# A decoder layer on one core: the queue that issues the transfers of the stored operands

## The chip, the cores and the metric

The kernel runs on one core of one Trainium2 chip. The metric is the device time of one execution in microseconds (us). The core has TensorE (PE in the profile; its weight loads are PEld), VectorE (DVE), ScalarE (ACT) and GpSimd (POOL). SyncE (SP) computes nothing here and issues most transfers. SP and GpSimd each issue transfers in the order of their own queue. An instruction at the head of a queue that waits for a semaphore holds up all that stand behind it.

## The reference

One layer of a hybrid decoder in float32, on x of 1024 tokens by 1024 features, with a memory of 256 tokens:

```
h = LN1(alpha*x + 0.5 * (silu(x@wg1) * (x@wu1)) @ wd1)      # FFN 1, inner width 2816
h = LN2(alpha*h + [HGRN2(h) ; spatial_gate(h)] @ w_out)      # token mixers
h = LN3(alpha*h + attention(h, LN(mem)) @ xa_w_o)            # 4 heads, 256 memory tokens
out = LN4(alpha*h + 0.5 * (silu(h@wg2) * (h@wu2)) @ wd2)     # FFN 2, the same form
```

## The kernel before

Every matmul operand is split into a rounded high part (ACT, L114) and a low remainder (DVE, L115), and each product is three matmuls: high by high, low by high and high by low (`mm3`, L137 to L139). Each FFN runs through its 22 column blocks of 128 in pairs. For a pair it loads four 512 KB weight tiles, two of the gate (`wg_f_r`) and two of the up projection (`wu_f_r`), and forms sums of them on DVE (L498 to L501), because each projection is done with seven block products in place of eight (`strassen`). A pair is thus 14 products of 12 matmuls of 128x128 by 128x512. The results leave PSUM through ACT (L528, L531, L533) and DVE, and SP stores combinations of them in DRAM (`lops`, L626 to L629). The next pair's weights are loaded and split while this pair is multiplied. A raw weight tile has 3 buffers (tag `raw`), a high part 6 (tag `whi`) and a low part 5.

Beside the pairs of FFN 1 runs a flow of its own, `later` (L926), which makes ready what later stages read: 14 tiles for the output projection of attention (`sq_xa`, called items 0 to 13 here) and 4 tiles of FFN 2's weights (`f_ops`). The flow is `prepare` (L281). For each item it does this, and then rests for 16 us of the program's own reckoning, in which a product counts as 2.6 us:

- the raw tile is in a buffer of which there is one (`load`, L283, tag `pre`, tiles `pr_xa` and `pr_f`);
- ACT writes its high part `ph_xa` (L293) and the negative of that, `pn_xa` (L294), both into buffers of the tag `whi`, the pool from which the weights of the pairs take theirs;
- both are stored to DRAM (L296), and the next item's raw tile is loaded (L286);
- an adding transfer adds the raw operand in DRAM onto the stored negative, which leaves the low part (L301);
- for items 0 to 7, a step of the sums of blocks follows (`square_operands`, L261): an even item copies one 512x512 block to a sum in DRAM, and the next odd item adds another block to it, each in two halves (L269). The sums 7, 6, 4 and 5 are made in this order; sum 6 begins as a copy of sum 7, and sum 4 as a copy of sum 6. Later items load these sums as raw tiles.

`pinned` keeps instructions of one engine in the program's order. The rest is placed by a scheduler, which sets the order of every queue when the kernel is built. All transfers of `prepare` but the loads of the four FFN 2 tiles stand on GpSimd's queue. There are 16 `nc.gpsimd.dma_start` halves at L269, 14 loads at L286, 36 stores at L296 and 30 adding transfers at L301, each of 512 KB or of a part of that. The weight loads, and all else, stand on SP's queue.

Of the kernel before, what the change touches and what calls it, by code (L numbers as in the profile page):

```python
# [8 lines left out]
F32 = mybir.dt.float32  # L9
# [25 lines left out]
def hybrid_layer_kernel(ctx: ExitStack, tc: tile.TileContext, a, out):  # L35
    nc = tc.nc
# [10 lines left out]
    def gt(name, shape=(P, 1024), dtype=F32):  # L47
        return gpool.tile(list(shape), dtype, tag="g", name=name)
# [209 lines left out]
    pinned = tc.keep_in_program_order  # L258
    probe = {}

    def square_operands(w, ops, name):  # L261

        wb = w.rearrange("(kb k) (db d) -> kb db k d", kb=2, db=2)
        sums, steps = {}, []
        halves = [slice(i * 2 * P, (i + 1) * 2 * P) for i in range(2)]

        def step(dst, src, **op):
            for rows in halves:
                pinned(nc.gpsimd.dma_start(dst[rows], src[rows], **op))  # L269

        for p, b in ((1, (0, 0)), (2, (1, 0)), (3, (1, 1))):
            sums[p] = wb[b[0], b[1]]
        for p, first, b in ((7, 3, (0, 1)), (6, 7, (0, 0)), (4, 6, (1, 0)), (5, 1, (0, 1))):
            sums[p] = dram.tile([HALF, HALF], F32, name=f"sum_{name}{p}")
            steps.append(partial(step, sums[p], sums[first]))
            steps.append(partial(step, sums[p], wb[b[0], b[1]], accum_op=ALU.add))
        todo = [(sums[p][2 * n * P:2 * (n + 1) * P].rearrange("(i p) d -> p i d", p=P), ops[p - 1, n],
                 f"{name}_{p}{n}") for p in (1, 2, 3, 7, 6, 4, 5) for n in range(2)]
        return todo, steps

    def prepare(todo, steps):  # L281

        def load(k):  # L283
            src, _, name = todo[k]
            raw = wpool.tile(list(src.shape), F32, tag="pre", bufs=1, name=f"pr_{name}")
            pinned((nc.gpsimd if src.shape[1] == 2 else nc.sync).dma_start(raw, src))  # L286
            return raw

        raw = load(0)
        yield 16  # L290
        for k, (src, dst, name) in enumerate(todo):
            hi, neg = (wpool.tile(list(src.shape), F32R, tag="whi", bufs=6, name=f"p{i}_{name}") for i in "hn")
            pinned(nc.scalar.activation(hi, raw, AF.Copy))  # L293
            pinned(nc.scalar.activation(neg, hi.bitcast(F32), AF.Copy, scale=-1.0))  # L294
            for d, t in zip(dst, (hi, neg)):
                pinned(nc.gpsimd.dma_start(d, t.bitcast(F32)))  # L296
            if k + 1 < len(todo):
                raw = load(k + 1)
            for i in range(0, src.shape[1], 2):
                part = slice(i, i + 2)  # L300
                pinned(nc.gpsimd.dma_start(dst[1][:, part], src[:, part], accum_op=ALU.add))  # L301
            if steps:
                steps.pop(0)()
            yield 16

    def fetch_parts(src, name):
        hi = wpool.tile(list(src[0].shape), F32R, tag="whi", bufs=6, name=f"{name}_h")
# [323 lines left out]
    def down(wd, res_src, gb, bb, dst, make_xT, name):  # L631
# [73 lines left out]
        def pair(ps, when):  # L705

            bank = {p: [(ps_tr if j and t > 1 else ps_mm)(f"dp_{name}_{p}_{t}") for t in range(4)]
                    for j, p in enumerate(ps)}
            for k, _ in steps(ps):
                ahead(3)  # L710
                rh, rl, lh, ll = ready.pop((ps, k))
                for j, p in enumerate(ps):
                    l = SLOT[p] - min(SLOT[q] for q in ps)
                    for t in range(4):
                        ts = slice(t * P, (t + 1) * P)
                        mm3(bank[p][t], lh[:, l, ts], ll[:, l, ts], rh[:, j, :], rl[:, j, :],
                            k == 0, k == nk - 1)
                tick(5.2)
                if k in when:
                    prepare(when[k])  # L720
            ahead(2)
            return [bank[p] for p in ps]
# [203 lines left out]
    def later():  # L926
        yield 40

        pinned(nc.gpsimd.tensor_scalar(sm("begun", [P, 1]), probe["b"], 1.0, None, op0=ALU.mult))
        todo, steps = [], []  # L930
        for n, w in (("xa", a["xa_w_o"][0]),):
            t, s = square_operands(w, sq_ops[n], n)
            todo += t
            steps += s
        todo += [(wcol(w, f), f2_ops[i, f], f"f2{i}{f}") for f in range(2)
                 for i, w in enumerate((a["ffn2_w_gate"][0], a["ffn2_w_up"][0]))]
        yield from prepare(todo, steps)
# [451 lines left out]
    for j in range(2):  # L1389
        for i, (hi, lo) in enumerate(((kTh[j].rearrange("p c m -> p (c m)"),  # L1390
                                       kTl[j].rearrange("p c m -> p (c m)")), (vmh[j], vml[j]))):
            t = gt(f"kv{i}{j}")
# [72 lines left out]
```

## Time and profile before

| | |
|---|---|
| Time, median of 3 runs | 2069.17 us (2065.11 to 2072.62) |
| The profiled execution's own time | 2069.69 us |
| Its span, first to last instruction | 2068.0 us |
| PE busy | 2017.1 us (98%) |
| DVE, ACT and POOL busy | 1488.4, 916.2 and 176.8 us |
| Mean granted TensorE clock | 0.989 |
| Queue of SP (q1) | 315.75 MB |
| Queue of GpSimd (q0) | 44.05 MB |

In a row of the timeline stand the start, the duration, the engine, the line and what is written from what. In brackets stands how long the engine sat idle before it, and which instruction's end let it go; "issue" there means that the profile shows nothing that it waited for. In the table of waits stand the total, the number of waits and the longest one. Buffer numbers are left out of the names, so that FFN 1 and FFN 2 both appear as `f`; FFN 1's pairs lie between 62 and about 520 us.

### The profile page before, as it was taken

How to read it: one execution, taken by the hardware profiler on the slowest of the kernel's cores; microseconds unless marked ns; L12 is line 12 of the kernel's file. 1: busy time of each engine (PE TensorE's matmuls, PEld its weight loads, DVE VectorE, ACT ScalarE, POOL GpSimd, SP SyncE). 2: the span in 40 equal slices, each digit the busy share in tenths (PEclk: the TensorE clock that was granted, in tenths of full speed). 3: DMA queues.
4: the chain of work that ended last, by engine and by line, in shares of the span. 5: the costliest groups of instructions: out<-in, count | busy, mean ns of one | idle time of the engine just before them, and what ended most of it. 6: DMA issues, size and time to landing. Idle time of an engine off the chain costs nothing.

```text
span 2068.0 us, 25498 instructions
## 1 busy us (share of the span) xinstructions
PE 2017.1 (98%) x9598; PEld 1686.4 (82%) x9598; DVE 1488.4 (72%) x2238; ACT 916.2 (44%) x1279; POOL 176.8 (9%) x245
## 2 busy tenths in 40 slices
PE   8999879999999999999999999999999999999998
PEld 8888658878787888888888888888888888888886
DVE  5977456748767876785797765478776776776688
ACT  6634334434343537746754434334423333344442
POOL 0011221120000220100011100001000000000021
PEclk9999989999999999999999999999999999999999
DMA  8369987855877753123225643464233332377874
GB/s 262 116 200 254 248 226 211 244 158 168 302 266 274 258 163 87 50 82 90 64 84 189 226 130 115 165 244 162 87 113 97 97 114 95 107 240 280 290 264 167
DMA packets 265371, 361.41 MB, mean 175 GB/s; under 512 B 16224, under 2 KB 160224, under 8 KB 265184
## 3 DMA queue, kind: packets, MB, share of 16 engines
q1 hardware_dynamic: 247008, 315.75, 45.7%
q0 software_dynamic: 18240, 44.05, 8.9%
q8 instruction: 75, 1.23, 0.2%
q14 instruction: 48, 0.39, 0.1%
HBM read 267.99 MB, written 109.58 MB: 183 GB/s over the span
## 4 chain that ended last, share of the span: by engine, by line
PE 68%; DVE 3%; DMA 1%; issue 1%; POOL 1%; ACT 0%; SPq 0%; POOLq 0%; DVEq 0%; ACTq 0%
PE dp_f L137 6%; PE dp_f L138 5%; PE dp_f L139 5%; PE st_gf L138 3%; PE st_uf L138 3%; PE st_uf L137 3%; PE st_gf L137 3%; PE st_gf L139 3%; PE st_uf L139 3%; PE psl L1167 2%; PE paq L137 1%; PE paq L138 1%; PE paq L139 1%; PE acc_mx L137 1%; PE acc_mx L139 1%; PE acc_mx L138 1%
## 5 line engine op out<-in xcount | busy, mean ns | idle before, releaser
L138 PE MATMUL dp_f<-wd_f_l,ah_f 128*128 128x512 f32 x552 | 214.3, 391 | 0.0
L137 PE MATMUL dp_f<-wd_f_h,ah_f 128*128 128x512 f32 x552 | 209.6, 392 | 3.9 <-ACT ah_f L114 3.9
L139 PE MATMUL dp_f<-wd_f_h,al_f 128*128 128x512 f32 x552 | 206.1, 390 | 0.6 <-DVE al_f L115 0.6
L137 PEld LDWEIGHTS dp_f<-wd_f_h,ah_f 128*128 128x128 f32 x552 | 104.2, 189 | 26.1 <-ACT ah_f L114 4.7
L139 PEld LDWEIGHTS dp_f<-wd_f_h,al_f 128*128 128x128 f32 x552 | 103.6, 188 | 22.7 <-DVE al_f L115 1.5
L138 PEld LDWEIGHTS dp_f<-wd_f_l,ah_f 128*128 128x128 f32 x552 | 104.2, 189 | 21.7
L114 ACT ACTIVATE wd_f_h<-wd_f_r 128x1024 fp32r<-128x1024 f32 x72 | 73.1, 1021 | 94.3 <-DVE wd_f_r L650 35.7
L114 ACT ACTIVATE ah_f<-ar_f 128x1024 fp32r<-128x1024 f32 x72 | 73.3, 1020 | 71.4 <-DMA ar_f<-lops 67.2
L115 DVE TENSOR_TENSOR al_f<-ar_f,ah_f 128x1024 fp32r<-128x1024 f32 x72 | 84.5, 1174 | 27.8 <-ACT ah_f L114 27.3
L115 DVE TENSOR_TENSOR wd_f_l<-wd_f_r,wd_f_h 128x1024 fp32r<-128x1024 f32 x72 | 84.2, 1174 | 10.7 <-ACT wd_f_h L114 10.7
L115 DVE TENSOR_TENSOR wu_f_l<-wu_f_r,wu_f_h 128x1024 fp32r<-128x1024 f32 x42 | 51.2, 1219 | 47.6 <-ACT wu_f_h L114 47.6
L137 PE MATMUL st_uf<-xh,wu_f_h 128*128 128x512 f32 x168 | 66.3, 394 | 14.0 <-ACT wu_f_h L114 14.0
L774 POOL TENSOR_SCALAR nm_f<-nm_f 128x1 f32<-128x1 f32 x8 | 10.6, 1330 | 780.8 <-ACT xl L773 780.8
L114 ACT ACTIVATE wu_f_h<-wu_f_r 128x1024 fp32r<-128x1024 f32 x42 | 44.1, 1051 | 49.6 <-issue 31.0
L138 PE MATMUL st_uf<-xl,wu_f_h 128*128 128x512 f32 x168 | 65.9, 392 | 0.0
L137 PE MATMUL st_gf<-xh,wg_f_h 128*128 128x512 f32 x168 | 65.4, 389 | 0.0
L138 PE MATMUL st_gf<-xl,wg_f_h 128*128 128x512 f32 x168 | 65.4, 389 | 0.0
L139 PE MATMUL st_uf<-xh,wu_f_l 128*128 128x512 f32 x168 | 64.9, 390 | 0.0
L139 PE MATMUL st_gf<-xh,wg_f_l 128*128 128x512 f32 x168 | 64.7, 389 | 0.0
L530 DVE TENSOR_TENSOR top_uf<-bot_uf,st_uf 128x512 f32<-128x512 f32 x21 | 14.4, 687 | 59.4 <-PE st_uf L139 46.7
L114 ACT ACTIVATE wg_f_h<-wg_f_r 128x1024 fp32r<-128x1024 f32 x42 | 44.2, 1052 | 21.9 <-PE st_gf L138 15.1
L115 DVE TENSOR_TENSOR wg_f_l<-wg_f_r,wg_f_h 128x1024 fp32r<-128x1024 f32 x42 | 51.2, 1220 | 3.2 <-ACT wg_f_h L114 2.9
(504 smaller groups left out, 6015.5 us busy)
## 6 DMA issues: line engine op xcount, KB each, us to landing
ar_f<-lops SPq DMA_DIRECT2D x66, 512.0 KB, 5.3
wd_f_r<-in_ffn_w_down_dram SPq DMA_DIRECT2D x56, 512.0 KB, 5.0
wg_f_r<-in_ffn_w_gate_dram SPq DMA_DIRECT2D x42, 512.0 KB, 3.8
wu_f_r<-in_ffn_w_up_dram SPq DMA_DIRECT2D x42, 512.0 KB, 3.9
wd_mx_r<-in_w_out_dram SPq DMA_DIRECT2D x24, 512.0 KB, 4.2
lops<-bot_gf SPq DMA_DIRECT2D x21, 512.0 KB, 2.8
lops<-top_uf SPq DMA_DIRECT2D x21, 512.0 KB, 4.5
lops<-bot_uf SPq DMA_DIRECT2D x21, 512.0 KB, 5.1
```

What stands on the lines that cost most here:

```text
L114: order(nc.scalar.activation(hi, src, AF.Copy))
L115: order(nc.vector.tensor_tensor(lo, src, hi.bitcast(F32), op=ALU.subtract))
L137: nc.tensor.matmul(ps, lh, rh, start=first, stop=False, skip_group_check=more)
L138: nc.tensor.matmul(ps, lh, rl, start=False, stop=False, skip_group_check=more)
L139: nc.tensor.matmul(ps, ll, rh, start=False, stop=last, skip_group_check=more)
L530: nc.vector.tensor_tensor(t0, b0, product(2), op=ALU.add)
L774: nc.gpsimd.tensor_scalar(nmean, nmean, -1.0 / D, None, op0=ALU.mult)
L1167: nc.tensor.matmul(psl[:m, (i * NC2 + c) * 64:(i * NC2 + c + 1) * 64] .rearrange("p (n b) -> p n b", b=B), e[:, :m], blk(e, B)[:, :, 1, :] ...
```

## The change

GpSimd keeps the adding transfers alone, at L269 and L301. The plain copies of the sums, all loads of raw tiles and the stores of both parts go to SP's queue. Between ACT's two conversions and the stores the flow now rests for 4, and at the end of an item for 12 instead of 16. Behind L294 the changed kernel's line numbers are one higher.

```diff
         def step(dst, src, **op):
             for rows in halves:
-                pinned(nc.gpsimd.dma_start(dst[rows], src[rows], **op))
+                pinned((nc.gpsimd if op else nc.sync).dma_start(dst[rows], src[rows], **op))
...
-            pinned((nc.gpsimd if src.shape[1] == 2 else nc.sync).dma_start(raw, src))
+            pinned(nc.sync.dma_start(raw, src))
...
             pinned(nc.scalar.activation(neg, hi.bitcast(F32), AF.Copy, scale=-1.0))
+            yield 4
             for d, t in zip(dst, (hi, neg)):
-                pinned(nc.gpsimd.dma_start(d, t.bitcast(F32)))
+                pinned(nc.sync.dma_start(d, t.bitcast(F32)))
...
             if steps:
                 steps.pop(0)()
-            yield 16
+            yield 12
```

In the built program 58 transfers move from GpSimd's queue to SP's: 36 stores, 14 loads and 8 half copies. The order of PE's instructions is the same as before; on ACT and DVE a few neighbours of FFN 1 change places.

The first place is GpSimd's queue in the items 7 to 9. `sum_xa_1188` is sum 5, and a wait for DMASW is a wait for an earlier transfer of GpSimd, one for DMAHW for one of SP, one for Activation for ACT. Before:

```order
L296 DMA sq_xa<-ph_xa_2193 128x1024 [waits DMASW3_49,Activation_49]
L296 DMA sq_xa<-pn_xa_2194 128x1024 [waits DMASW4_49,Activation_49]
L286 DMA pr_xa_2199<-sum_xa_1186 128x2x512 [waits DMASW7_49,DMASW5_49]
L301 DMA sq_xa<-sum_xa_1185 256x1x512 [waits DMASW4_49]
L269 DMA sum_xa_1188<-in_xa_w_o_dram 256x512 [waits DMASW1_49]
L269 DMA sum_xa_1188<-in_xa_w_o_dram 256x512 [waits DMASW2_49,DMASW0_49]
L296 DMA sq_xa<-ph_xa_2329 128x1024 [waits Activation_49]
L296 DMA sq_xa<-pn_xa_2330 128x1024 [waits Activation_49]
L286 DMA pr_xa_2335<-sum_xa_1186 128x2x512 [waits DMASW5_49,DMASW3_49]
```

The same queue now, at the same items:

```order
L302 DMA sq_xa<-sum_xa_1185 256x1x512 [waits DMAHW1_49,DMASW5_49]
L269 DMA sum_xa_1188<-in_xa_w_o_dram 256x512 [waits DMAHW4_49,DMASW6_49]
L269 DMA sum_xa_1188<-in_xa_w_o_dram 256x512 [waits DMAHW5_49,DMASW7_49]
L302 DMA sq_xa<-sum_xa_1186 256x1x512 [waits DMAHW7_49,DMASW0_49]
L302 DMA sq_xa<-sum_xa_1186 256x1x512 [waits DMAHW5_49,DMASW1_49]
```

The stores of items 7 and 8 and the load of item 9, the last row of the fence before, no longer stand behind the two halves that are added to sum 5. They are now on SP's queue, whose rows at item 8 are these:

```order
L123 DMA wg_f_12_1_r<-in_ffn_w_gate_dram 128x8x128 [waits DMAHW6_49,DMAHW4_49,DVE_49]
L297 DMA sq_xa<-ph_xa_2329 128x1024 [waits DMAHW5_49,Activation_49]
L630 DMA lops<-top_gf_8_2026 128x512 [waits DVE_49]
L297 DMA sq_xa<-pn_xa_2330 128x1024 [waits DMAHW7_49,Activation_49]
L286 DMA pr_xa_2363<-sum_xa_1186 128x2x512 [waits DMAHW2_49,DMAHW0_49]
L629 DMA lops<-bot_gf_8_2027 128x2x512 [waits DMAHW1_49,DVE_49]
```

There they stand between SP's own loads and stores, and wait for ACT and for SP's own earlier transfers.

The second place is SP's queue at item 2, while FFN 1's third pair is multiplied. `wg_f_6` and `wu_f_6` are weights of the fourth pair. Before:

```order
L628 DMA lops<-bot_gf_2_1155 128x2x512 [waits DMAHW4_49,DVE_49]
L123 DMA wg_f_6_1_r<-in_ffn_w_gate_dram 128x8x128 [waits DMAHW5_49,DMAHW0_49,DVE_49]
L626 DMA lops<-top_uf_2_1289 128x2x512 [waits DMAHW6_49,DVE_49]
L627 DMA lops<-bot_uf_2_1290 128x2x512 [waits DMAHW7_49,DVE_49]
L123 DMA wg_f_6_2_r<-in_ffn_w_gate_dram 128x8x128 [waits DMAHW1_49,DVE_49]
L123 DMA wu_f_6_1_r<-in_ffn_w_up_dram 128x8x128 [waits DMAHW3_49,DVE_49]
```

And now, where `sum_xa_1185` is sum 7 and `sum_xa_1186` sum 6:

```order
L123 DMA wg_f_6_1_r<-in_ffn_w_gate_dram 128x8x128 [waits DMAHW6_49,DVE_49]
L627 DMA lops<-top_uf_2_1289 128x2x512 [waits DMAHW7_49,DVE_49]
L628 DMA lops<-bot_uf_2_1290 128x2x512 [waits DMAHW0_49,DVE_49]
L297 DMA sq_xa<-ph_xa_1537 128x1024 [waits DMAHW1_49,Activation_49]
L297 DMA sq_xa<-pn_xa_1538 128x1024 [waits DMAHW2_49,Activation_49]
L286 DMA pr_xa_1598<-in_xa_w_o_dram 128x2x512 [waits DMAHW3_49]
L269 DMA sum_xa_1186<-sum_xa_1185 16x8192 [waits DMAHW4_49,DMASW2_49]
L269 DMA sum_xa_1186<-sum_xa_1185 16x8192 [waits DMAHW5_49,DMASW3_49]
L123 DMA wg_f_6_2_r<-in_ffn_w_gate_dram 128x8x128 [waits DMAHW6_49,DVE_49]
L123 DMA wu_f_6_1_r<-in_ffn_w_up_dram 128x8x128 [waits DMAHW7_49,DVE_49]
```

Two stores that wait for ACT, a load, and two half copies that each wait for one of GpSimd's adding transfers now stand ahead of the two weight loads.

## The prediction, made before the result was known

> **What bounds the kernel now.** I read the page first, then PE's waits, then the timeline of PE, and from each of PE's waits back through ACT to GpSimd's queue. The page's first part says that PE is all but full:
>
> ```profile
> PE 2017.1 (98%) x9598; PEld 1686.4 (82%) x9598; DVE 1488.4 (72%) x2238; ACT 916.2 (44%) x1279; POOL 176.8 (9%) x245
> ```
>
> So only PE's idle time, and time in which PE runs slowly, can be won. PE's table of waits has three long rows that name FFN's pairs (total, times, longest):
>
> ```profile
> PE st_uf L137 <- ACT wu_f_h L114: 14.0, 1, 14.0
> PE st_uf L137 <- ACT bot_gf L533: 6.3, 1, 6.3
> PE st_gf L137 <- ACT bot_gf L528: 4.6, 1, 4.6
> ```
>
> They sum to 24.9 us, each a single wait. What they cost in all shows in the timeline of PE, in the first matmul of a pair:
>
> ```profile
> 186.12 0.39 PE L137 MATMUL st_gf<-xh,wg_f_h 128*128 128x512 f32 x1
> 224.20 0.39 PE L137 MATMUL st_gf<-xh,wg_f_h 128*128 128x512 f32 x1
> 271.82 0.39 PE L137 MATMUL st_gf<-xh,wg_f_h 128*128 128x512 f32 x1
> 325.57 0.39 PE L137 MATMUL st_gf<-xh,wg_f_h 128*128 128x512 f32 x1
> ...
> 439.81 0.39 PE L137 MATMUL st_gf<-xh,wg_f_h 128*128 128x512 f32 x1
> 484.38 0.39 PE L137 MATMUL st_gf<-xh,wg_f_h 128*128 128x512 f32 x1
> ```
>
> The first two rows enclose an undisturbed pair: 224.20 - 186.12 = 38.08 us. The pairs from 224.20, 271.82 and 439.81 take 47.62, 53.75 and 44.57 us, which is 9.54, 15.67 and 6.49 us too much, **31.7 us together**. The 6.8 us beyond the 24.9 are slow matmuls after each wait, as the granted clock in the windows of these three pairs and of an undisturbed fourth one shows (seventh figure, the one behind POOL; then the share of the DMA engines and GB/s):
>
> ```profile
> 224.20:271.80 47.60, 40.71 (x169) 32.61 (x168) 29.07 (x39) 17.59 (x22) 9.68 (x13) 0.93 0.94 268
> 271.80:325.60 53.80, 39.75 (x170) 32.47 (x169) 30.93 (x42) 17.91 (x23) 11.50 (x15) 0.87 0.84 209
> 439.80:484.40 44.60, 40.03 (x170) 32.60 (x169) 28.94 (x38) 15.81 (x22) 10.47 (x10) 0.96 0.51 126
> 363.70:401.70 38.00, 38.00 (x169) 31.50 (x168) 29.55 (x40) 18.62 (x23) 5.96 (x8) 1.00 0.88 246
> ```
>
> **Why PE waits there.** ACT works in order, and in each of the three places it stands still for a transfer of `prepare`. ACT's timeline, with the conversion that each transfer belongs to:
>
> ```profile
> 232.01 1.06 ACT L293 ACTIVATE ph_xa<-pr_xa 128x1024 fp32r<-128x1024 f32 x1 [0.33 <-DMA pr_xa<-sum_xa]
> ...
> 254.76 1.06 ACT L114 ACTIVATE wu_f_a_h<-wu_f_sa 128x1024 fp32r<-128x1024 f32 x1 [8.57 <-DMA sq_xa<-ph_xa]
> ...
> 274.53 1.06 ACT L294 ACTIVATE pn_xa<-ph_xa 128x1024 fp32r<-128x1024 f32 x1
> ...
> 301.93 1.06 ACT L293 ACTIVATE ph_xa<-pr_xa 128x1024 fp32r<-128x1024 f32 x1 [18.43 <-DMA pr_xa<-sum_xa]
> ...
> 441.64 1.05 ACT L293 ACTIVATE ph_f<-pr_f 128x1024 fp32r<-128x1024 f32 x1
> ...
> 459.27 1.06 ACT L114 ACTIVATE wu_f_h<-wu_f_r 128x1024 fp32r<-128x1024 f32 x1 [15.48 <-DMA f_ops<-ph_f]
> ```
>
> Twice a weight's high part needs a `whi` buffer that the store of `ph` still holds, and once, for 18.43 us, ACT waits for the next raw tile. GpSimd's timeline shows when these transfers were issued:
>
> ```profile
> 245.49 0.92 POOL L296 DMA_DIRECT2D sq_xa<-ph_xa  x1
> ...
> 281.25 0.92 POOL L269 DMA_DIRECT2D sum_xa<-in_xa_w_o_dram  x1 [8.03 <-issue]
> 290.19 0.90 POOL L269 DMA_DIRECT2D sum_xa<-in_xa_w_o_dram  x1 [8.02 <-issue]
> ...
> 297.75 0.74 POOL L286 DMA_DIRECT2D pr_xa<-sum_xa  x1 [5.54 <-issue]
> ...
> 454.60 1.05 POOL L296 DMA_DIRECT2D f_ops<-ph_f  x1
> ```
>
> The store of the tile that was ready at 232.01 + 1.06 = 233.1 goes out at 245.5, 12.4 us late. The raw tile's buffer was free by 275.6, and its load goes out at 297.7, 22 us late. The store ready at 442.7 goes out at 454.6, 11.9 us late. In the middle case the rows ahead of the late load are two adding transfers, before each of which GpSimd stood for 8 us; in the other two the store is late in the same way, behind the additions of the item before.
>
> **The change, part by part.** *Stores and loads to SP (the gain).* I test each wait with the longest landing in the trace, in case the transfers are no faster on SP. The landing lines are those of the tiles `sq_xa`, `sum_xa` and `wg_f_r`, in this order:
>
> ```profile
> DMA to landing us min/median/max: 2.9/5.3/10.1
> ...
> DMA to landing us min/median/max: 4.1/7.1/8.8
> ...
> DMA to landing us min/median/max: 3.5/3.8/10.6
> ```
>
> The rows of SP that stand just ahead of the moved ones in the first two places are stores of `lops`:
>
> ```profile
> 240.69 0.36 SPq L626 DMA_DIRECT2D lops<-top_uf  x1
> ...
> 277.72 0.34 SPq L629 DMA_DIRECT2D lops<-top_gf  x1
> ```
>
> - *Second wait (14.0 us).* In the new order the load stands behind the store of `lops<-top_gf`, so at 278.4 at the latest, after it and the other part's store. It lands by 282.5 to 287.2 (4.1 to 8.8 us). ACT wanted the tile at 301.93 - 18.43 = 283.5, so it waits 0 to 3.7 us. PE idled 14.0 of ACT's 18.43 us, so 4.4 us of such a wait are covered. It goes.
> - *Third wait (4.6 us).* The store goes out at 442.7 and lands by 448.0 (5.3) to 452.8 (10.1). ACT asked at 443.8, so it waits 4.2 to 9.0 in place of 15.48 us, and 15.48 - 4.6 = 10.9 us are covered. It goes.
> - *First wait (6.3 us).* ACT asked at 254.76 - 8.57 = 246.2, and 2.3 us are covered. The store now stands behind `lops<-top_uf` of 240.69, issued by 241.1, so it lands at 246.4 to 251.2: a wait of 0.2 to 5.0, of which PE would feel 0 to 2.7 us. I take 0, what the median gives. It goes.
>
> So all three go, with the slow matmuls after them: -31.7 us. What is late next is nothing that the trace shows: the pair of 363.70 has all its stores and loads on the same DMA engines, and its PE is busy in 38.00 of 38.00 us.
>
> *More work on SP (cost 0).* 58 issues at the 0.37 us that a 512 KB issue takes (the row of 167.27 below) are 21.5 us, over some 330 us in which SP has about eight issues of its own in a pair. In the new order each transfer also waits for the one eight places ahead in SP's queue (DMAHW0 to 7). With about 15 transfers in a pair that one is some 20 us old, and the longest landing is 10.6.
>
> *New waits on SP (cost 0 to 14, taken 1).* What SP now waits for holds up its weight loads. A store waits for ACT, which had finished near that place in the queue anyhow. The two half copies of sum 6 from sum 7, and of sum 4 from sum 6, wait for GpSimd's additions. The rows for the first case, from the timelines of ACT, POOL, SP and DVE:
>
> ```profile
> 141.66 1.06 ACT L294 ACTIVATE pn_xa<-ph_xa 128x1024 fp32r<-128x1024 f32 x1
> ...
> 149.47 1.10 POOL L301 DMA_DIRECT2D sq_xa<-in_xa_w_o_dram  x1 [4.98 <-DMA sq_xa<-pn_xa]
> 157.79 0.93 POOL L269 DMA_DIRECT2D sum_xa<-in_xa_w_o_dram  x1 [7.22 <-issue]
> 165.81 0.89 POOL L269 DMA_DIRECT2D sum_xa<-in_xa_w_o_dram  x1 [7.10 <-issue]
> ...
> 167.27 0.37 SPq L123 DMA_DIRECT2D wg_f_r<-in_ffn_w_gate_dram  x1
> ...
> 178.71 0.69 DVE L498 TENSOR_TENSOR wg_f_sa<-wg_f_r 128x512 f32<-128x512 f32 x1
> ...
> 182.56 1.22 DVE L115 TENSOR_TENSOR wg_f_l<-wg_f_r,wg_f_h 128x1024 fp32r<-128x1024 f32 x1
> ```
>
> Item 1's negative is ready at 142.7, its store lands 5.3 later at 148.0, and three additions follow, spaced 8.3 and 8.0 us as they were: the last starts at 164.3 and lands at 171.4 (7.1). SP stands till then, and the load `wg_f_6_2` behind it, of 167.27 before, is 4.1 us late. It lands at 175.2 (3.8) to 182.0 (10.6). DVE wants it at 178.71, so it is in time or 3.3 us late. Late by 3.3, the low part of the pair's first weights, now done at 183.8, is done at 187.1, where the pair that starts at 186.12 needs it after two matmuls: about half a microsecond of PE. With the longest store (10.1 for 5.3) and the widest spacing (290.19 - 281.25 = 8.9, twice) 6.3 us are added, 7 in all. Twice that is 14 us, the upper bound. I take half a microsecond at each, as nearer to the median rows.
>
> The Trainium skill (DMA: Bandwidth & Descriptors, Anatomy of one DMA) has the DMA engines wait for no semaphore: any wait is on the issuing sequencer, ahead of dispatch. By that rule the cover of a prefetched weight is all that stands between these copies and PE; the trace agrees in that GpSimd's stores went out only when the rows ahead of them had.
>
> **The sum.** 2069.69 (the profiled execution's own time, 0.5 us above the median of 2069.17, so I leave it as it is) - 31.7 + 1 = **2039 us**.
>
> **The rivals.**
>
> *SP's block gives part of it back.* The copies, or a store behind `lops`, cost what the upper bounds say: 14 + 2.7 us, so up to 2055, and from 2046 on. For it: landings of weight loads up to 10.6 us. Against it: the medians leave 3.5 us of cover.
>
> *The DMA engines are full, and the queue is not the cause.* Then all transfers are as late from SP, and the time stays at 2069. For it: a share of 0.94 and 0.84 in two of the bad pairs. Against it: the third has 0.51, the undisturbed one 0.88, and the late tile of 297.75 had not been issued. The Trainium skill (DMA: Bandwidth & Descriptors, Rules for kernel authors) says that spreading transfers over several issuing engines brings no bandwidth, as all use the same 16 DMA engines, and saves issue time alone. If issue time were only the 0.9 us of a row the change would be worth nothing by that rule; the rows show a queue that stands for 8 us at a time.
>
> *Slower: the additions become a chain that SP waits for.* Items 0 to 7 hold four additions in two items, and two items pass in a pair of 38.08 us: up to 9.5 us each they keep pace. At 12 us each, if SP's transfers between them slow them, the first copies are released 11 us later than in my sum, 7 us past DVE's need, some 4 us of PE. The next pair's lag 48 - 38 = 10 us more, some 17 us of PE, and sum 5's additions and the stores behind them as much again. That is about 40 us for the 31.7 won: 2078. It decides from about 11 us on. Against it: spacings of 8.0 to 8.9 in the trace, while GpSimd's queue also carried the stores.
>
> That the move does not take place is no rival: the order of the queues shows all 58 transfers on SP.
>
> **How the numbers follow.** 0.3% is 6.2 us, about what a measurement of this kernel can tell from no change. My forecast 0.74 (2036 to 2046), part given back 0.14 (2046 to 2055), no change 0.06, slower 0.06. The first two are faster by more than 0.3%: 0.88. The range begins at 2034, the sum with no new cost (2038) less the 4 us by which the runs shown lie off their median, and ends at 2054, nearly all of the second case.
>
> **What would show it.** Right: PE's three waits are gone, all pairs of FFN 1 take 38.08 us, ACT has no wait of over 10 us for `pr_xa` or for a store of `ph`, and GpSimd's additions are still spaced by about 8 us. SP's waits gain rows for the copies at L269. Wrong: a pair of over 38.5 us, with ACT or DVE waiting for a weight load; or additions spaced by over 9.5 us; or waits of the same length with the stores issued on time, which would mean the DMA engines.

## The result, and the profile after

| | before | after |
|---|---|---|
| Time, median of 3 runs | 2069.17 us (2065.11 to 2072.62) | 2037.76 us (2032.09 to 2038.50) |
| The profiled execution's own time | 2069.69 us | 2037.76 us |
| Its span | 2068.0 us | 2036.0 us |
| Mean granted TensorE clock | 0.989 | 0.995 |

The ratio is 0.9841, with a 95% interval of 0.9802 to 0.9881: faster, by 1.2 to 2.0%. Between the two profiled executions the span is 32.0 us shorter. Where these 32.0 us lie is read from PE's first matmul of each pair. In the code after the change, lines behind L294 are one higher.

The first part of the page after the change, and the rows of its DMA queues (packets, MB, share of 16 engines):

```profile
PE 2009.1 (99%) x9598; PEld 1681.2 (83%) x9598; DVE 1490.1 (73%) x2238; ACT 917.3 (45%) x1279; POOL 140.7 (7%) x187
...
q1 hardware_dynamic: 257216, 346.16, 50.5%
q0 software_dynamic: 10336, 13.63, 4.6%
```

PE's busy time fell by 8.0 us (2017.1 to 2009.1) for the same 9598 matmuls. These are slow matmuls that are gone (the granted clock is 0.995 instead of 0.989). The rest of the 32 us was idle time. 30 MB went from q0 to q1. PE's waits after the change (total, times, longest):

```profile
PE dp_f L137 <- DVE db_f L798: 4.8, 2, 3.0
PE st_uf L137 <- ACT wu_f_h L114: 2.7, 1, 2.7
...
PE st_uf L137 <- DVE bot_gf L536: 0.9, 1, 0.9
PE dp_f L137 <- ACT ah_f L114: 0.6, 1, 0.6
```

The waits of 14.0, 6.3 and 4.6 us have become 2.7, 0.9 and none. The timeline of PE shows what a pair takes now:

```profile
185.29 0.39 PE L137 MATMUL st_gf<-xh,wg_f_h 128*128 128x512 f32 x1
...
223.37 0.39 PE L137 MATMUL st_gf<-xh,wg_f_h 128*128 128x512 f32 x1
...
262.66 0.39 PE L137 MATMUL st_gf<-xh,wg_f_h 128*128 128x512 f32 x1
...
305.66 0.39 PE L137 MATMUL st_gf<-xh,wg_f_h 128*128 128x512 f32 x1
...
343.74 0.39 PE L137 MATMUL st_gf<-xh,wg_f_h 128*128 128x512 f32 x1
```

The pairs from 223.37 and 262.66 take 39.29 and 43.00 us, still 1.21 and 4.92 us too long, 6.1 together. All later ones take 38.08, also the one in which the third stall had been, and so do the three ahead of them. FFN 1's first pair takes longer in every kernel here (47.73 us before, 47.14 now) and is left out of what is said of pairs. So the three pairs gave 31.7 - 6.1 = 25.6 us. ACT's timeline shows what is left:

```profile
246.18 1.06 ACT L114 ACTIVATE wu_f_a_h<-wu_f_sa 128x1024 fp32r<-128x1024 f32 x1 [3.39 <-DMA sq_xa<-ph_xa]
...
264.32 0.63 ACT L114 ACTIVATE wg_f<-wg_f_r 128x512 fp32r<-128x512 f32 x1 [4.65 <-DMA sq_xa<-ph_xa]
...
281.39 1.06 ACT L293 ACTIVATE ph_xa<-pr_xa 128x1024 fp32r<-128x1024 f32 x1 [7.05 <-DMA pr_xa<-sum_xa]
```

At these three places ACT stood 8.57, 3.04 and 18.43 us before. SP's timeline has the load for which ACT waits at 281.39:

```profile
268.78 0.53 SPq L297 DMA_DIRECT2D sq_xa<-ph_xa  x1
271.50 0.34 SPq L630 DMA_DIRECT2D lops<-top_gf  x1
271.93 0.56 SPq L297 DMA_DIRECT2D sq_xa<-pn_xa  x1
272.59 0.66 SPq L286 DMA_DIRECT2D pr_xa<-sum_xa  x1
```

ACT had asked at 281.39 - 7.05 = 274.3. The load had gone out at 272.59, behind the store of `top_gf`, and landed 8.73 us later. The copies at L269 hold SP up as the prediction said, the first ones until 171.6:

```profile
162.02 9.56 SPq L269 DMA_DIRECT2D sum_xa<-sum_xa  x2
171.68 0.53 SPq L123 DMA_DIRECT2D wg_f_r<-in_ffn_w_gate_dram  x1
...
202.06 10.22 SPq L269 DMA_DIRECT2D sum_xa<-sum_xa  x2
```

GpSimd, with the adding transfers alone, is no quicker:

```profile
234.91 0.91 POOL L269 DMA_DIRECT2D sum_xa<-in_xa_w_o_dram  x1 [8.04 <-DMA lops<-top_gf]
243.89 0.91 POOL L269 DMA_DIRECT2D sum_xa<-in_xa_w_o_dram  x1 [8.08 <-issue]
254.93 1.06 POOL L302 DMA_DIRECT2D sq_xa<-sum_xa  x1 [10.13 <-issue]
```

The spacing is 9.0 and 11.0 us here. Over all 512 KB additions that wait for nothing but the addition ahead it is 6.5 to 11.0 us, and 6.8 to 9.6 before. Each addition here goes out 0.31 us after the one ahead has landed (at 243.58 and 254.62). The windows of three pairs (clock, share of the DMA engines and GB/s stand last):

```profile
147.20:185.30 38.10, 38.10 (x170) 31.54 (x169) 24.03 (x33) 16.26 (x20) 3.44 (x4) 1.00 0.96 263
223.40:262.70 39.30, 38.45 (x170) 31.39 (x169) 28.98 (x39) 16.34 (x20) 3.94 (x4) 1.00 0.96 263
262.70:305.70 43.00, 40.27 (x170) 32.51 (x169) 31.63 (x42) 19.30 (x24) 5.01 (x5) 0.96 0.95 270
```

At the same load of the DMA engines, the first pair runs undisturbed and the other two don't.

**A gain that was not forecast: the gap behind the last pair.** Matched matmul by matmul, PE gains another 5.6 us where FFN 1's last pair gives way to its down projection: 3.8 us of a gap, and the rest of slow matmuls behind it. Before, from the timelines of DVE, ACT and PE:

```profile
496.68 0.68 DVE L498 TENSOR_TENSOR wu_f_sa<-wu_f_r 128x512 f32<-128x512 f32 x1
...
525.17 1.06 ACT L114 ACTIVATE ah_f<-ar_f 128x1024 fp32r<-128x1024 f32 x1 [7.07 <-DMA ar_f<-lops]
...
526.28 0.73 PE L137 MATMUL dp_f<-wd_f_h,ah_f 128*128 128x512 f32 x1 [3.66 <-ACT ah_f L114]
```

After, from those of DVE and ACT:

```profile
464.30 0.68 DVE L499 TENSOR_TENSOR wu_f_sa<-wu_f_r 128x512 f32<-128x512 f32 x1
...
492.23 1.06 ACT L114 ACTIVATE ah_f<-ar_f 128x1024 fp32r<-128x1024 f32 x1 [0.53 <-DMA ar_f<-lops]
```

DVE sums the last pair's up weights 12.3 us after that pair's first matmul (496.68 - 484.38) before, and 6.3 after it (464.30 - 457.98) now. The third stall, one pair earlier, had left ACT and DVE 6 us behind. The pair itself has cover for that, the down projection after it has none. Two waits on `db_f`, at the ends of the down projections, also changed, by -2.5 us (FFN 1) and +3.2 us (FFN 2). The sum of PE's offsets is -0.8 (ahead of the three pairs) - 25.6 - 5.6 - 2.5 + 3.2 = -31.3 us, and the spans differ by 32.0.

### The profile page after: what moved, and what is told of

Its sections match the earlier page's. It is cut to its first block, busy times and chain, and to the rows that moved or that the text cites. A ratio compares the mean times of both kernels' runs of the same rounds, so it can differ in the third digit from the quotient of the medians.

```text
span 2036.0 us, 25494 instructions
## 1 busy us (share of the span) xinstructions
PE 2009.1 (99%) x9598; PEld 1681.2 (83%) x9598; DVE 1490.1 (73%) x2238; ACT 917.3 (45%) x1279; POOL 140.7 (7%) x187
## 3 DMA queue, kind: packets, MB, share of 16 engines
q0 software_dynamic: 10336, 13.63, 4.6%
## 4 chain that ended last, share of the span: by engine, by line
PE 82%; DMA 5%; DVE 4%; issue 1%; ACT 1%; POOL 0%; SPq 0%; POOLq 0%; DVEq 0%; ACTq 0%
PE dp_f L137 6%; PE dp_f L138 6%; PE dp_f L139 6%; PE st_uf L139 5%; PE st_uf L138 5%; PE st_uf L137 5%; PE st_gf L139 5%; PE st_gf L138 5%; PE st_gf L137 5%; PE psl L1168 2%; DMA wg_f_r<-in_ffn_w_gate_dram 1%; PE paq L137 1%; PE paq L139 1%; PE paq L138 1%; PE acc_mx L137 1%; PE acc_mx L138 1%
## 5 line engine op out<-in xcount | busy, mean ns | idle before, releaser
L529 ACT ACTIVATE bot_gf<-st_gf 128x512 f32<-128x512 f32 x21 | 12.5, 594 | 93.1 <-PE st_gf L139 93.1
```

Source lines behind the costliest of these rows:

```text
L529: nc.scalar.activation(b0, product(1), AF.Copy)
```

## The experiments

*Theory:* GpSimd's queue stands before each adding transfer until the one ahead has landed, and the stores and loads behind it are late. *Rivals:* the DMA engines are full and any queue would be late; or it is the new pause and order, not the queue. Each ratio is to the kernel before on the same chip, with its 95% interval.

**One part of the change alone.** Only the eight stores of FFN 2's tiles moved:

```diff
-                pinned(nc.gpsimd.dma_start(d, t.bitcast(F32)))
+                pinned((nc.gpsimd if src.shape[1] == 2 else nc.sync).dma_start(d, t.bitcast(F32)))
```

> The kernel before, with only the eight stores of FFN 2's four tiles on SP's queue; the other 50 moved transfers stay on GpSimd's. Queue theory: the stalls in the pairs from 224.20 and 271.82 stay, the one from 439.81 (6.49 us) goes. If the gap between FFN 1's last pair and its down projection (5.6 us shorter after the change) is lag that this third stall left on ACT and DVE, it goes as well: 2069 - 12 = 2057. Rival, that the gap is another matter: 2069 - 6.5 = 2063. Rival, that the DMA engines are the cause: 2069, the stall stays.

Measured: 2055.02 us, ratio 0.9932 (0.9920 to 0.9944), 14 us for eight stores. From PE's timeline, the pair in which the third stall was:

```profile
438.07 0.39 PE L137 MATMUL st_gf<-xh,wg_f_h 128*128 128x512 f32 x1
...
476.15 0.39 PE L137 MATMUL st_gf<-xh,wg_f_h 128*128 128x512 f32 x1
```

38.08 us: that stall is gone, the other two are there (pairs of 46.28 and 53.30 us), and the gap behind the last pair costs 5.6 us less.

The other 50 transfers moved, the eight stores left on GpSimd's queue (L269 and the loads as in the change, no pause, and this at the stores):

```diff
-                pinned(nc.gpsimd.dma_start(d, t.bitcast(F32)))
+                pinned((nc.sync if src.shape[1] == 2 else nc.gpsimd).dma_start(d, t.bitcast(F32)))
```

> The kernel before, with stores, loads and copies of the attention projection's 14 items on SP's queue, the eight stores of FFN 2's tiles left on GpSimd's. Queue theory: the first two stalls shrink as after the full change (to 1.2 and 4.9 us), the third and the gap behind the last pair stay as before: 2038 + 12 = 2050. Rival, that the gap is another matter and varies by itself: 2044. Rival, that the DMA engines are the cause: the first two stalls stay too, 2069.

Measured: 2045.64 us, ratio 0.9888 (0.9872 to 0.9905). The pairs from 224.48 and 262.79 take 38.31 and 41.50 us. The third stall and the wait behind the last pair are there, in PE's timeline:

```profile
418.53 0.39 PE L137 MATMUL st_gf<-xh,wg_f_h 128*128 128x512 f32 x1
...
463.54 0.39 PE L137 MATMUL st_gf<-xh,wg_f_h 128*128 128x512 f32 x1
...
505.18 0.69 PE L137 MATMUL dp_f<-wd_f_h,ah_f 128*128 128x512 f32 x1 [3.40 <-ACT ah_f L114]
```

The pair takes 45.01 us. So the gap goes with the third stall and stays with it: it is a part of that stall's price, 6.5 + 5.6 us. The time lies between the two expectations: the first two stalls left 4.0 us instead of 6.1 (0.4 of it in the pair from 186.02), and the ends of the two down projections came to -5.4 and +3.5 us. Those waits on `db_f` differ from one execution to the next (below); whether a part of them belongs to the change isn't separated.

The 36 stores alone (loads and copies on GpSimd, no pause):

```diff
-                pinned(nc.gpsimd.dma_start(d, t.bitcast(F32)))
+                pinned(nc.sync.dma_start(d, t.bitcast(F32)))
```

> The kernel before, with the 36 stores alone on SP's queue; loads and copies stay on GpSimd's, behind the additions. Queue theory: the waits for a buffer that a store holds go (first stall 9.5, third 6.5, gap 5.6), the wait for the late load stays (second stall, 15.7): about 2069 - 21.6 = 2047.5. If freeing the queue of stores also lets the load out earlier, down to 2040. DMA engines as the cause: 2069.

Measured: 2048.79 us, ratio 0.9899 (0.9885 to 0.9912), close to the 2047.5 expected. The third stall and the gap are gone, and the second stays (a pair of 54.34 us), as its load still stands behind the additions. The first shrinks from 9.54 to 4.93 us only, where I expected it to go, so that the total agrees in part by luck: the trace gains another 4.3 us at the end of FFN 1's down projection.

The 14 loads alone:

```diff
-            pinned((nc.gpsimd if src.shape[1] == 2 else nc.sync).dma_start(raw, src))
+            pinned(nc.sync.dma_start(raw, src))
```

> The kernel before, with the 14 loads alone on SP's queue; stores and copies stay on GpSimd's. Queue theory: the first and third stalls stay; at the second the raw tile comes in time, but its high part's store stands behind the same two additions, so that ACT meets a held buffer instead of a missing tile: the stall shrinks but does not go, 2058 to 2066. If the load alone was the cause there: 2069 - 15.7 = 2053.5. DMA engines as the cause: 2069.

Measured: 2073.72 us, ratio 1.0016 (1.0002 to 1.0030): no gain at all, where the queue theory as I had stated it gave 3 to 11 us. The second stall did shrink, from 15.67 to 12.61 us, but the first grew from 9.54 to 13.66, and all pairs are 36.9 us too long, against 31.7. SP's table of waits and ACT's timeline have the reason:

```profile
SPq L286 <- ACT ph_xa L293: 53.8, 12, 15.4
```

```profile
262.01 1.06 ACT L114 ACTIVATE wu_f_a_h<-wu_f_sa 128x1024 fp32r<-128x1024 f32 x1 [11.95 <-DMA sq_xa<-ph_xa]
```

A load waits until ACT has emptied the one raw buffer. ACT is held up by stores that are still on GpSimd's queue, so SP stands up to 15.4 us at the load, with the pairs' weight loads behind it. Moved alone, the loads carry GpSimd's delay into SP's queue.

**The pause and the order on SP.** The changed kernel with the load ahead of the pause and the stores:

```diff
+            if k + 1 < len(todo):
+                raw = load(k + 1)
             yield 4
             for d, t in zip(dst, (hi, neg)):
                 pinned(nc.sync.dma_start(d, t.bitcast(F32)))
-            if k + 1 < len(todo):
-                raw = load(k + 1)
```

> The changed kernel, with the next raw tile's load issued right behind ACT's two conversions, ahead of the pause of 4 and of the two stores. Order theory (what is left of the second stall, 4.9 us, is the load standing behind a store that waits for DVE's top_gf): the load goes out some 3.5 us earlier, ACT's wait of 7.05 us shrinks to about 3.5, less than the 4.4 that are covered, and the pair takes 38.1 to 39: 4 us below the changed kernel on this chip, ratio about 0.980 to before. Rival, that the load of the DMA engines (share 0.94 to 0.96, landings of 8 to 14 us) sets what is left: the same time as the changed kernel, ratio about 0.984.

Measured: 2038.84 us, ratio 0.9836 (0.9807 to 0.9864), no gain to be seen. The pair with the second stall takes 39.42 us, little more than the 38.1 to 39 expected, but another one, from 185.29, takes 40.70. With the pair between them the three are 5.7 us too long in all, so the loss has moved and not gone.

The changed kernel without the pause:

```diff
-            yield 4
             for d, t in zip(dst, (hi, neg)):
...
-            yield 12
+            yield 16
```

> The changed kernel with the rest of 16 at the end of an item, as before the change, and none between the conversions and the stores. Theory (the pause keeps SP from standing at a store until ACT is done): SP waits longer at the stores of ph, weight loads behind them are late, and 2 to 10 us come back: ratio 0.985 to 0.989. Rival, that weight loads have cover enough: no difference to the changed kernel, ratio 0.984.

Measured: 2034.77 us, ratio 0.9822 (0.9796 to 0.9847). In the profiled execution the pairs are 8.1 us too long in all, 6.5 of them in the pair with the second stall, but the pause makes no difference that the times can tell. So the 2 to 10 us expected of it did not come, and the gain is the queue's.

**Why GpSimd stands.** The kernel before, with each adding transfer a plain copy of the same bytes on the same queue. The low parts and sums that are stored are then not those of the layer:

```diff
-                pinned(nc.gpsimd.dma_start(dst[1][:, part], src[:, part], accum_op=ALU.add))
+                pinned(nc.gpsimd.dma_start(dst[1][:, part], src[:, part]))
...
-            steps.append(partial(step, sums[p], wb[b[0], b[1]], accum_op=ALU.add))
+            steps.append(partial(step, sums[p], wb[b[0], b[1]]))
```

> The kernel before, order of all queues unchanged, with every adding transfer of the preparation made a plain copy of the same size, still on GpSimd's queue (the stored low parts and sums are thus not the right ones). Theory A (GpSimd's queue takes a transfer of 256 KB only when the one before has landed, whatever it does): GpSimd still stands before each, by the shorter landing of a copy, and at least the second stall stays: 2055 to 2069. Theory B (adding itself blocks the queue): no standing of 8 us, the stalls and the gap behind the last pair go, about 2069 - 37 = 2032.

Measured: 2029.63 us, ratio 0.9796 (0.9767 to 0.9825). All pairs from the second on take 38.08 us. GpSimd's timeline has three such transfers in a row:

```profile
252.59 0.69 POOL L301 DMA_DIRECT2D sq_xa<-sum_xa  x1 [2.40 <-DMA sq_xa<-pn_xa]
253.19 0.68 POOL L269 DMA_DIRECT2D sum_xa<-in_xa_w_o_dram  x1
254.81 0.57 POOL L269 DMA_DIRECT2D sum_xa<-in_xa_w_o_dram  x1 [0.95 <-issue]
```

They go out 0.6 and 1.6 us apart. So plain transfers on GpSimd's queue cost nothing here; what costs is that adding ones stand ahead of others. (The size of 256 KB in the expectation is wrong: 22 of the 38 adding transfers move 512 KB, the 16 of FFN 2's tiles 128 KB, which makes the 13.63 MB of q0.)

The kernel before with more room for the descriptors of GpSimd's transfers, and one buffer fewer of the tag `g` to pay for it:

```diff
-    gpool = ctx.enter_context(tc.tile_pool(name="gpool", bufs=22))
+    gpool = ctx.enter_context(tc.tile_pool(name="gpool", bufs=21))
...
-    nc = _bacc.Bacc("TRN2", target_bir_lowering=False, num_devices=1, dynamic_dma_scratch_size=1024)
+    nc = _bacc.Bacc("TRN2", target_bir_lowering=False, num_devices=1, dynamic_dma_scratch_size=4096)
```

> The kernel before with 4096 instead of 1024 bytes per partition set aside for the descriptors of GpSimd's transfers, and 21 instead of 22 buffers of the tag g to make room; GpSimd's queue is in the same order. Theory A (GpSimd stands because the space for descriptors is taken by the transfers ahead): no standing of 8 us between additions, stores and loads go out on time, the three stalls and the gap go: about 2032, plus what the missing buffer costs in later stages. Theory B (adding transfers go one at a time whatever the space): spacing of 8 us and all three stalls stay in FFN 1's pairs, 2069 or more.

Measured: 2054.15 us, ratio 0.9908 (0.9881 to 0.9936). GpSimd's timeline, with three adding transfers in the first two rows:

```profile
265.52 1.09 POOL L301 DMA_DIRECT2D sq_xa<-sum_xa  x1 [3.35 <-DMA sq_xa<-pn_xa]
266.14 2.31 POOL L269 DMA_DIRECT2D sum_xa<-in_xa_w_o_dram  x2
268.96 0.59 POOL L296 DMA_DIRECT2D sq_xa<-ph_xa  x1 [0.51 <-ACT ph_xa L293]
270.06 0.55 POOL L296 DMA_DIRECT2D sq_xa<-pn_xa  x1 [0.51 <-ACT pn_xa L294]
270.60 0.73 POOL L286 DMA_DIRECT2D pr_xa<-sum_xa  x1
```

They go out 0.6 us apart and adding still. So it was the room for descriptors that made GpSimd stand. The work of DVE doesn't explain the difference: DVE is busy for 1488.4 us in the kernel before, and for 1489.2 and 1489.7 us in these two, with the same 2238 instructions. The third stall and the gap behind the last pair are gone. One pair is still 7.7 us too long (45.82, from 265.71) and three others 0.5 to 1.2, with waits of ACT that the kernel before doesn't have, the longest of them this:

```profile
284.67 0.60 ACT L531 ACTIVATE top_gf<-st_gf 128x512 f32<-128x512 f32 x1 [14.43 <-DMA lops<-top_gf]
```

`top_gf` has the tag `g`, of which this kernel has one buffer fewer, so this is most likely a wait for that buffer; PE's order in later stages differs too. How much of the remaining time is due to it isn't separated.

**What is left of the stalls.** The changed kernel with the low part formed on DVE, and only the eight adding halves of the sums left:

```diff
-            pinned(nc.scalar.activation(neg, hi.bitcast(F32), AF.Copy, scale=-1.0))
+            nc.vector.tensor_tensor(neg, raw, hi.bitcast(F32), op=ALU.subtract)
...
-            for i in range(0, src.shape[1], 2):
-                part = slice(i, i + 2)
-                pinned(nc.gpsimd.dma_start(dst[1][:, part], src[:, part], accum_op=ALU.add))
```

> The changed kernel with the low part of each stored tile formed on DVE (raw less high part, as for the weights of the pairs) and stored from there: ACT's negation and the 30 adding transfers at L302 are left out, only the 8 halves that add to the sums stay on GpSimd. Theory (what is left of the stalls, 6.1 us, are transfers that land late while adding transfers take the DMA engines): the pairs take 38.1 us, DVE gains 18 x 1.2 = 22 us beside PE, time 6 us below the changed kernel, ratio about 0.981. Rival, that DVE (30 of 38 us busy in a pair) becomes what PE waits for: no gain, ratio 0.984 or above.

The same edit in the kernel before, all on GpSimd's queue as it was:

> The kernel before, stores, loads and copies on GpSimd's queue as they were, with the same edit on the low part: 30 of the 38 adding transfers are gone, the 8 for the sums stay ahead of stores and loads. Queue theory: the third stall and the gap behind the last pair go (12.1 us), of the first two some 8 of 25 us stay, since one of the three adding transfers ahead of the late rows is gone: about 2070 - 29 = 2041, ratio 0.986. Rival, that any adding transfer ahead is enough for the old stalls: 2070 - 12 = 2058, ratio 0.994.

The changed kernel with plain copies in place of the adding transfers (`accum_op` left out as above; it too stores other low parts and sums):

> The changed kernel, order of all queues unchanged, with every adding transfer made a plain copy of the same size (the stored low parts and sums are thus not the right ones). Theory (late landings under adding transfers are what is left): all pairs take 38.1 us, about 6 us and up to 10 below the changed kernel: ratio 0.980. Rival, that SP's added duties (waits for the additions, more issues) cost what is left: the pairs from 223.37 and 262.66 stay 1 to 5 us too long, ratio 0.984.

The changed kernel again, without an edit:

> The changed kernel itself, unaltered, to see how far its pairs and the ends of the down projections differ from one profiled execution to the next. If the rest of the two stalls is of the change, the pairs that took 39.29 and 43.00 us take 38.3 to 40 and 41 to 45 again and the third stall is gone again; the waits of 3 to 4 us at the ends of the down projections come and go by themselves. Ratio about 0.984 to before.

Measured, all on one chip, with 2071.14 us for the kernel before:

| kernel | us | ratio | pairs too long, in all |
|---|---|---|---|
| changed, low part on DVE | 2029.28 | 0.9800 (0.9780 to 0.9821) | 0 |
| before, low part on DVE | 2029.58 | 0.9801 (0.9778 to 0.9825) | 0 |
| changed, plain copies | 2029.03 | 0.9797 (0.9774 to 0.9820) | 0 |
| changed, again | 2030.99 | 0.9807 (0.9782 to 0.9832) | 1.5 us |

The repeat is needed to read the other three. Its pairs, from PE's timeline:

```profile
224.52 0.39 PE L137 MATMUL st_gf<-xh,wg_f_h 128*128 128x512 f32 x1
...
262.66 0.39 PE L137 MATMUL st_gf<-xh,wg_f_h 128*128 128x512 f32 x1
...
302.21 0.39 PE L137 MATMUL st_gf<-xh,wg_f_h 128*128 128x512 f32 x1
```

They take 38.14 and 39.55 us, where the first execution had 39.29 and 43.00. The same kernel thus loses 1.5 to 6.1 us in these two pairs, and its PE waits on `db_f` came to 2.9 us here against 4.8. In the three kernels with eight adding transfers or none, nothing is lost in the pairs. The row of GpSimd's queue in the kernel with plain copies, to be set beside that of the changed kernel above, shows what adding costs:

```profile
q0 software_dynamic: 3936, 13.63, 2.1%
```

For the same 13.63 MB in the same 38 transfers, adding takes 272 packets each where a copy takes 104 on average, and 4.6% of the DMA engines' time in place of 2.1%. The windows of the same two pairs in the first kernel of the table have a lower share of the DMA engines (last figure but one), 0.85 and 0.58, where the changed kernel's have 0.96 and 0.95:

```profile
222.60:260.70 38.10, 38.10 (x170) 31.55 (x169) 29.21 (x38) 15.74 (x19) 1.79 (x2) 1.00 0.85 249
260.70:298.80 38.10, 38.10 (x170) 31.56 (x169) 28.27 (x38) 14.07 (x18) 0.00 (x0) 1.00 0.58 198
```

That kernel also moves fewer bytes; with plain copies, which move the same, the two pairs have 0.90 and 0.70. The landings tell more than the share, as the repeat has 0.95 and 0.97 and loses little. The median landing of SP's transfers issued between 223 and 300 us is 8.15 us in the changed kernel and 7.65 in the repeat, against 4.09 in the first kernel of the table and 4.92 with plain copies. So the record points to late landings beside adding transfers, as the theory for the third kernel of the table had it. Its rival isn't excluded: SP's waits for the additions at L269, 18.6 us in all in the changed kernel, are gone in these two kernels too. Either way the size is small: on one chip the four times agree within 0.1%, well inside their intervals. None is shown to beat the change.

The second kernel of the table is a miss of mine. I expected 8 of the first two stalls' 25 us to stay, since two adding transfers in a row still stood ahead of stores and loads. From its GpSimd timeline:

```profile
258.49 0.89 POOL L269 DMA_DIRECT2D sum_xa<-in_xa_w_o_dram  x1 [6.34 <-issue]
259.07 0.90 POOL L296 DMA_DIRECT2D sq_xa<-ph_xa  x1
263.71 0.56 POOL L296 DMA_DIRECT2D sq_xa<-pn_xa  x1 [3.75 <-DVE pn_xa L294]
267.76 0.73 POOL L286 DMA_DIRECT2D pr_xa<-sum_xa  x1 [3.49 <-issue]
```

The queue stands 6.34 us once and 3.49 us again, and between 200 and 300 us no wait of ACT for a transfer is over 0.91 us. One standing ahead of the late rows is covered here. That several in a row are needed to pass what the pairs cover (2.3, 4.4 and 10.9 us in the prediction) fits this, but no run shows it by itself.

## Why the prediction was right, point by point

- **The bound and the place.** PE's idle time in three pairs, through ACT, to late transfers on GpSimd's queue: right, and shown by the parts. The third stall goes with eight stores alone, and the first two shrink to 4.0 us with the other 50 transfers. Why GpSimd stood, the prediction left open; it is the room for descriptors.
- **The DMA engines as the cause.** Wrong for the three stalls: the changed kernel has a pair of 38.10 us at a share of 0.96, and moving eight stores between queues won 14 us. The Trainium skill (DMA: Bandwidth & Descriptors, Issuing engines are not separate DMA queues) says that all issuers use the same 16 engines and that several issuers save issue time alone. The trace agrees on bandwidth (263 to 270 GB/s after, 268 in the fullest pair before), but what was saved is far more than the 0.9 us of an issue: a queue that stands for 8 us at a time is a cost of its own, worth 33 us here. For the few microseconds that are left, the landings suggest that the load of the engines does count.
- **"All three go."** The third went. Of the first, 0 to 2.7 us were to stay and 0 were taken: 1.2 stayed in one execution, 0.1 in the other. For the second I gave ACT a wait of 0 to 3.7 us, covered by 4.4; it was 7.05 (5.17 in the repeat), and PE lost 4.9 and 1.5 us. The cover was right, as 7.05 - 4.4 is the 2.7 us that PE waited; the rest are slow matmuls. The landing was in my bounds (8.73 of 4.1 to 8.8). What failed is the time of issue: I let the row of SP ahead of the load, the store of `top_gf`, move with the pair. ACT asks 9.2 us earlier than before (283.5 to 274.3), but the store goes out only 6.2 us earlier (277.72 to 271.50), as ACT's work ahead of it waits for other stores: at 264.32 for one of `ph`, 4.65 us in place of 3.04, which is 1.6 of the 3 us, the rest having come before. The load behind is thus 3 us late against ACT.
- **More issues on SP, cost 0:** right. The pairs from 147.21 and 185.29 take 38.08 us.
- **The copies' waits, 0 to 14, taken 1:** they cost 0. SP stood at the first until 171.6 (171.4 forecast); the load behind it was in time. The upper bound of 14 took 8.9 us as the widest spacing, where the trace before has 9.6 (189.79 to 199.35); nothing came of it.
- **Additions still 8 us apart; over 9.5 would mean wrong.** They are 6.5 to 11.0 us apart with SP's transfers between them, and five of fourteen such spacings are over 9.5. So this sign of being wrong came, and the slower rival's condition (from about 11 us on) was nearly met. Its price did not come. The first run of three began at 145.45 instead of 149.47, as the store that it waits for was earlier. Its spacings were 6.6 and 8.7 us, and its last addition took 10.3 us to land instead of 7.1: the run ended at 171.1, where 171.4 was forecast. That the early start and the late landing cancel is luck. (At 12 us each from the prediction's start of 148.0, the run would end 12.6 us later than in its sum, where it says 11.)
- **The other signs.** ACT's longest wait for `pr_xa` or a store of `ph` in the pairs is 7.05 us, under the 10 named. Two pairs of over 38.5 us did come, but with ACT waiting for a store of `ph` and for the raw tile, not for a weight load.
- **What was left out:** the gap behind the last pair, 5.6 us of the third stall's price. I looked for what a stall costs in its own pair, not for where its lag is paid off.
- **The sum.** 2039 forecast, 2037.76 measured. That they agree to 1.3 us is luck, as the terms do not: 6.1 us were left of the stalls where I took none, the copies cost nothing where I took 1, and 5.6 us came from a gap that I did not see. The repeat on another chip gave a ratio of 0.9807 and 2030.99 us, which is below the range's 2034; the two intervals overlap, and a gain of 33 to 40 us is what the two ratios support.

## What to carry to other kernels

Where an in-order queue mixes transfers that can make it stand with others that an engine waits for, look at what is queued behind the standing ones: how full the DMA engines are doesn't answer that. Move the whole chain (here the stores as well as the loads): the loads moved alone carried the delay into the other queue. A stall's price is not complete until its lag is followed to the next place without cover.

## What the runs showed of the hardware

- An adding transfer from DRAM to DRAM holds back the next one on GpSimd's queue until it has landed, when 1024 bytes per partition are set aside for descriptors: in the changed kernel the next one goes out 0.31 us after the landing, 6.5 to 11.0 us after the one ahead for 512 KB. Those of 128 KB hold it too, 4.0 to 6.9 us apart. With 4096 bytes they go out 0.6 us apart. Two plain stores pass behind an addition at once (before the change, at 166.37 and 166.94 behind 165.81).
- Adding takes 272 packets, where a copy takes 144 for 512 KB and 48 for 128 KB, 104 on average here, and 2.2 times the DMA engines' time (4.6% against 2.1%).
- Landings stretch in a burst: in the changed kernel, the weight load issued at 243.54, behind seven other transfers within 6.3 us (237.28 to 241.81), took 14.2 us to land. Of FFN 1's 44 weight loads the median is 5.7 and the shortest 3.6.
